# Nine units of experts instead of ten, two of them late, and 415 GB/s in the plan: a hybrid decoder block on one core

## The chip, the cores and the metric

The kernel runs on one core of one Trainium2 chip. The metric is device microseconds of one execution. The kernel before took 536.14 us (median of 3 runs, 535.42 to 536.36); the profiled execution took 535.39 us, and its profile spans 533.4 us from the first to the last instruction, so that 2.0 us lie outside the span.

## What is computed

A decoder block on 256 tokens of width 1024, all float32. A mixer (forgetting attention and gated delta rule, with projections before and behind) comes first. Behind it comes a mixture of 32 experts, of which each token uses two, and behind that a gated embedding and a last norm. The change is all in the part with the experts:

```python
    for e in range(N_EXPERTS):
        hid = jax.nn.silu(t @ w_gate[e]) * (t @ w_up[e])
        out = out + gate[:, e:e + 1] * (hid @ w_down[e])
...
        ple_gate = jax.nn.sigmoid(rmsnorm(x, g_ple[i]) @ w_ple_gate[i])
        x = x + ple_gate * (p[i] @ w_ple_proj[i])
```

`gate` is zero but for two experts a token. Each expert has three weights of 1 MiB (`w_gate`, `w_up`, `w_down`), so that 96 MiB of the weights are the experts'.

## The kernel before, in words

**Places and units.** The kernel does not run every expert on all 256 tokens. It gives an expert a fixed number of places, gathers the tokens routed to it into them by a product with a one-hot matrix `G`, and scatters the result back by a product with the transposed matrix `C`. 128 places make a unit, the 128 columns of one pass through TensorE: two experts of 64 places each, or four of 32. `UNITS` lists them. Before there are ten: (0,1), (2,3), (4,5), (6,7) with 64 places an expert, then (8..11), (12..15) and so on to (28..31) with 32. The first six experts (`NSTAY`) are fixed numbers, since their weights are loaded ahead of the routing; the other numbers are places in an order by load, busiest first, and their weights are fetched by an indirect DMA on GpSimd's queue with the index `idx`. If an expert has more tokens than places, `flag` is set and a loop over all experts (`overflow`, behind a branch that every engine takes) does the rest.

**A unit's work on TensorE.** `group(i)` gathers the features of units 2i and 2i+1 together (`ga<-G,xx`, eight times four products of 128 x 256), and ScalarE copies them to `XT`. `gate_up` multiplies them by the unit's gate tiles (`gate<-`) and up tiles (`up<-`), `hidden` turns the result (`ga<-kp`) and multiplies it by the down tiles in two halves (`dn<-`; for late units the second half is written to `ga`). For an early unit `parts` scatters it into four sums (`sum<-yH,C` and `sum<-yL,C`).

**Late units.** From unit `UE` on a unit is late: units 7, 8, 9 before. Once the early units are summed, the gated embedding's product with `w_ple_gate` starts on those sums alone (`z_early`, `sum<-ra,xx` and the like, 32 products of 128 x 512), while the late units run. What a late unit adds is multiplied by `w_ple_gate` in its 64 places (`z_late`: 16 products `dn<-..,xx` and `gate<-..,xx` of 64 columns, four experts times `FEW` = 16 places), spread back (`z_spread`, `sum<-yH,G`) and added to x by itself (`late_spread`, `ga<-yH,C`). `UL` is the last unit, whose down product comes in three pieces (`last_down`) and whose chain ends the program. `z_early` waits for the gate product of unit `UE` to have been issued, so the first product of the first late unit always stands ahead of it on TensorE.

**Loads.** All weights pass through one ring of tiles of 1 MiB (`Ring`; 20 of them in this part, 17 once three are taken for the embedding), in one order: unit by unit, gate, up, down. A tile is asked for again when the product that read it last has been issued. `w_ple_gate` (four tiles, `wpg0` to `wpg3`) stands in that order right ahead of unit 7 (`WPG`). From unit `UE` - 1 on (`FIRST`) the down tiles come in pieces. SyncE issues the weights loaded ahead, GpSimd the rest, each strictly in order: a transfer whose tile is still in use holds up all behind it. ScalarE and VectorE multiply `w_ple_gate` by `g_ple` when it has come (`scaled`).

**What sets the order.** `Plan` runs the pieces of work as generators and advances the one that can start first by its own account of time, in which every operation has a cost (`Timed.cost`) and a transfer of n bytes takes n / 360e3 us (`Plan.load`). The account sets only the order in which each engine's instructions are written. Nearly all instructions carry line 77, that of the recording helper, so the tiles' names tell them apart.

Of the kernel before, what the change touches and what calls it, by code (L numbers as in the profile page):

```python
# [10 lines left out]
AF = mybir.ActivationFunctionType  # L11
OP = mybir.AluOpType
# [5 lines left out]
D = 1024  # L18
# [2 lines left out]
CAP = 64  # L21


NSTAY, NWIDE = 6, 8
UNITS = [list(range(e, e + 2)) for e in range(0, NWIDE, 2)] + [list(range(e, e + 4)) for e in range(NWIDE, E, 4)]
NU = len(UNITS)

WPG = (7, "g")

UE, UL = NU - 3, NU - 1  # L30

FEW = 16
FIRST = UNITS[UE - 1][0]
# [64 lines left out]
class Plan:  # L98
# [16 lines left out]
        self.end = max(self.end, self.free[key] + self.HOP)  # L115

    def load(self, since, nbytes):
        self.free["D"] = max(self.free["D"], since) + nbytes / 360e3
        return self.free["D"] + 2.0

    def tell(self, name, at=None):
# [2 lines left out]
    def after(self, name, n=1):  # L124
        return lambda: 0.0 if n <= 0 else self.told[name][n - 1] if len(self.told.get(name, ())) >= n else None
# [166 lines left out]
def hybrid_block(tc, x, p_t, w_in, w_o_fox, w_o_delta, w_out, w_gate, w_up, w_down, w_ple_gate,  # L292
# [84 lines left out]
    def K(name):  # L377
        a, b = KEEP[name]
        return kp[:, a:b]
# [849 lines left out]
    def last_tile():  # L1229
        for n in range(2):  # L1230
            yield after("sq1", n + 1)
            turned(1, n)
            yield
        logits(1, 0)
        yield
        yield after("sel")
        rank(0)
        logits(1, 1)
        yield
        yield from ffn_norm(1)  # L1240
        yield
        yield after("parts", 2)

        d = td[:, 0, :].rearrange("p (e s) -> p e s", s=CAP)
        for e in range(4):
            S.activation(d[:, e, :], K("slots"), AF.Square, scale=-1.0, bias=rk[:, 0, e:e + 1])
        S.activation(g0[:, 0].rearrange("p a (e s) -> p (a e) s", s=CAP), d, AF.Relu, scale=-1.0, bias=ones[:, 0:1])
        pr[1] = ps_t("mm")
        P.matmul(pr[1][:, 0:E], ones, sel[:, 0, :], start=True, stop=False)
        busy(6)  # L1250
        for k in range(4):
            gather(0, k)
        yield from route(1)
        rank(1)
        for k in range(4, 8):
            gather(0, k)
        busy(0)
        places(1)
        yield
# [71 lines left out]
    def half(i):  # L1331

        return (i % 2) ^ (i // 2 % 3 == 1)
# [64 lines left out]
    def order_experts():  # L1398
        yield after("sel", 2)
        pt = ps_t("dn")  # L1400
        for t in range(2):
            P.matmul(pt[0:32, 0:32], ones[:, 0:32], sel[:, t], start=t == 0, stop=t == 1)
        for t in range(2):
            P.matmul(pt[0:32, 32:33], sel[:, t], ones[:, 0:1], start=t == 0, stop=t == 1)
        yield
        keys, key, at = so[:, 0:32], so[:, 32:33], so[:, 33:34]
        V.scalar_tensor_tensor(key, pt[0:32, 32:33], 64.0, K("base")[0:32, 32:33], op0=OP.mult, op1=OP.add)
        V.scalar_tensor_tensor(keys, pt[0:32, 0:32], 64.0, K("base")[0:32, 0:32], op0=OP.mult, op1=OP.add)
        V.tensor_scalar(keys, keys, key, None, op0=OP.is_gt)
        V.tensor_reduce(at, keys, axis=AX.X, op=OP.add)  # L1410
        V.tensor_scalar(perm, K("places")[0:32, 0:32], at, None, op0=OP.is_equal)
        yield
        pt = ps_t("dn")
        P.matmul(pt[:, 0:32], K("places")[0:32, 32:33].to_broadcast([32, 128]), perm, start=True, stop=True)
        yield
        V.tensor_scalar(idx, pt[:, 0:32], K("places")[:, 33:34], None, op0=OP.add)
        tell("idx")
        V.tensor_scalar(rowf, pt[:, E - late:E], K("places")[:, 33:34], None, op0=OP.add)
        ring.index, ring.pieces = idx, idp
        ring.pump()  # L1420
        yield
        yield after("gate")
        yield from permute(rk, rkp, K("w_rt")[0:32, 0:256])
        tell("rkp")
        for (a, b), ix in idp.items():
            V.tensor_scalar(ix, rowf, 4.0 / (b - a), float(a // (b - a)), op0=OP.mult, op1=OP.add)
        yield after("weights")
        r = mo.tile([128, 2, 128], F32, name="hidT").rearrange("p k s -> p (k s)")[0:32]
        yield from permute(gr[:, :, :, 1], grp[:, :, :, 1], r)
        V.tensor_copy(grp[:, :, :, 0], gr[:, :, :, 0])  # L1430
        tell("grp")

        V.tensor_scalar(so[:, 34:35], at, NWIDE - 0.5, 32.0, op0=OP.is_lt, op1=OP.mult)
        V.tensor_scalar(so[:, 35:36], at, UNITS[UE][0] - 0.5, float(FEW - 32), op0=OP.is_gt, op1=OP.mult)
        V.tensor_tensor(so[:, 34:35], so[:, 34:35], so[:, 35:36], op=OP.add)
        yield
        pt = ps_t("sum00")
        P.matmul(pt[:, 0:32], so[:, 34:35].to_broadcast([32, 128]), ident[0:32, 0:32], start=True, stop=True)
        yield
        for t in range(2):  # L1440
            V.scalar_tensor_tensor(rko[:, t], rk[:, t], -32.0, pt[:, 0:32], op0=OP.add, op1=OP.subtract)
        V.tensor_reduce(big[:, 0:1], rko.rearrange("p t e -> p (t e)"), axis=AX.X, op=OP.max)
        yield
        pt = ps_t("sum00")
        P.transpose(pt[0:1, 0:128], big[:, 0:1], ident)
        yield
        V.tensor_reduce(big[0:1, 1:2], pt[0:1, 0:128], axis=AX.X, op=OP.max)
        V.tensor_scalar(flag, big[0:1, 1:2], 1.0, None, op0=OP.is_ge)
        tell("flag")
        yield  # L1450
# [16 lines left out]

    def group(i):

        yield after("rows", 2 * i - 2)  # L1470
        yield after("group", i - 1)
        yield after("G", i)
        g = mo.tile([128, 2, 2, 128], F32R, name="G") if i % 2 else g0
        X = XT[:, (slice(0, 2), slice(0, 3, 2), slice(1, 3))[i % 3]]
        wt = mo.tile([128, 2, 2], F32, name="wt", bufs=2)
        QD[i] = (g, wt)
        if i:
            yield after("rkp")
        for t in range(2) if i else (1,):
            yield after("rk", t + 1)  # L1480
            ranks = rkp if i else rk
            if half(2 * i) or 2 * i < UE <= 2 * i + 1:
                for a in range(2):
                    h = half(2 * i + a)
                    one_hot(g[:, t, h:h + 1], ranks[:, t], UNITS[2 * i + a])
            else:
                one_hot(g[:, t], ranks[:, t], UNITS[2 * i] + UNITS[2 * i + 1])
        tell("G")
        yield after("parts", 2)
        yield after("group", i)  # L1490
        yield after("gu", max(0, 2 * i - 1))
        for k in range(8):
            if i:
                yield turn()
                pt = ps_t("ga")[:, 0:256]
                n = 0
                for t in range(2):
                    for part in (xH, xL):
                        P.matmul(pt, part[:, t, k, :], g[:, t].rearrange("p a s -> p (a s)"), start=n == 0, stop=n == 3)
                        n += 1  # L1500
                plan.add(features_of(i, k, X, pt))
            else:
                gather(1, k)
                if k % 2:
                    for kk in (k - 1, k):
                        plan.add(features_of(i, kk, X, xb[kk // 2][:, kk % 2 * 256:kk % 2 * 256 + 256]))
                if k < 7:
                    continue
            yield
        yield after("grp" if i else "weights")  # L1510
        yield turn()

        pt = ps_t("ga")
        for a in range(2):
            u = UNITS[2 * i + half(2 * i + a)]
            m = 128 // len(u)
            for t in range(2):
                for o, e in enumerate(u):
                    P.matmul(pt[o * m:(o + 1) * m, 2 * a:2 * a + 2], g[:, t, a, o * m:(o + 1) * m].bitcast(F32), (grp if i else gr)[:, t, e, :],
                             start=t == 0, stop=t == 1, skip_group_check=True)  # L1520
        yield
        V.tensor_copy(wt.rearrange("p a b -> p (a b)"), pt[:, 0:4])
        tell("wt")
        tell("ga")
        tell("group")
        yield

    def features_of(i, k, X, pt):
        pt = pt.rearrange("p (a s) -> p a s", a=2)
        if True:  # L1530
            S.activation(X[:, :, k], pt, AF.Copy, scale=K("g_ffn")[:, k:k + 1])
        else:
            V.tensor_scalar(X[:, :, k], pt, K("g_ffn")[:, k:k + 1], None, op0=OP.mult)
        tell(f"X{i}")
        if i:
            tell("ga")
        yield
# [598 lines left out]
        nc.sync.dma_start(out[t * 128:(t + 1) * 128, 0:512], th)  # L2136
        yield

    for i in range(NU // 2):
        plan.add(group(i))  # L2140
    plan.add(add_x2())
    plan.add(order_experts())
# [95 lines left out]
```

## Time and profile before

| | |
|---|---|
| median of 3 runs | 536.14 us |
| profiled execution | 535.39 us |
| its span, and its mean granted TensorE clock | 533.4 us, 0.969 |
| TensorE products (PE) busy | 499.9 us, 94% of the span |
| VectorE, ScalarE, GpSimd busy | 229.7, 210.4, 133.9 us |
| moved by DMA | 141.25 MB |

PE is the row of products, PEld that of weight loads beside them. A float32 product shows as two records in the trace, a float32r product as one. Ends of products are modelled, so that a busy PE need not be a PE at its peak. In a table by stretches a row has the length, then for each engine busy us and instructions, and at the end the granted clock, the busy share of the 16 DMA engines and GB/s. In the chain of waits a row has start, length and what ran. In a timeline a row ends with the idle time before the first instruction and what ended it.

### The profile page before, as it was taken

To read this page: it belongs to the slowest core of one execution; us is meant where nothing else is said; L and a number is where in the kernel's file an instruction comes from. 1 tells how busy PE (TensorE), PEld (TensorE's weight loads), DVE (VectorE), ACT (ScalarE), POOL (GpSimd) and SP (SyncE) were. 2 spreads that over 40 slices of the span, in tenths; PEclk is the share of its full clock that TensorE was granted. 3 is DMA by queue.
4 is the path that set the end of the run, shared out by engine and by line. 5 is a ranking of instruction groups with operands and counts; after the bars stand their busy time and mean duration, and the time that the engine had idled before them with its cause. 6 is when DMAs were issued, how large, how long until landed. Compare 5 with 4: busy or idle time off the path is not lost. (4 is left out here: it accounts for less than half of the span.)

```text
span 533.4 us, 10476 instructions
## 1 busy us (share of the span) xinstructions
PE 499.9 (94%) x4375; PEld 351.0 (66%) x4375; DVE 229.7 (43%) x543; ACT 210.4 (39%) x475; POOL 133.9 (25%) x160
## 2 busy tenths in 40 slices
PE   7999999999999999979999999968986999989993
PEld 7999998899999999868555554423543444433441
DVE  3888689764655659584311111100123011012246
ACT  5576845566734545344231221203244011021144
POOL 5000551200000000061233324316444226425000
PEclk9999999999999999998999999979996999998997
DMA  8845533223098569875979999998999996985002
GB/s 343 347 159 167 192 119 115 67 89 131 7 402 303 170 225 423 314 289 188 358 278 384 367 378 340 373 396 308 412 421 416 421 412 227 421 349 201 1 1 79
DMA packets 25605, 141.25 MB, mean 265 GB/s; under 512 B 2625, under 2 KB 2897, under 8 KB 12626
## 3 DMA queue, kind: packets, MB, share of 16 engines
q0 software_dynamic: 14752, 86.01, 41.3%
q1 hardware_dynamic: 10658, 54.01, 27.0%
q8 instruction: 36, 0.59, 0.4%
q10 hardware_dynamic: 144, 0.52, 0.2%
q14 instruction: 15, 0.12, 0.1%
HBM read 139.46 MB, written 1.05 MB: 263 GB/s over the span
## 5 line engine op out<-in xcount | busy, mean ns | idle before, releaser
L77 PE MATMUL mm<-hH,ra 128*128 128x256 f32 x688 | 127.1, 284 | 0.0
L77 PEld LDWEIGHTS mm<-hH,ra 128*128 128x128 f32 x688 | 105.6, 188 | 1.5 <-issue 0.3
L77 PE MATMUL mm<-hL,ra 128*128 128x256 f32 x344 | 83.8, 281 | 0.5 <-DVE hL L77 0.5
L77 PEld LDWEIGHTS mm<-hL,ra 128*128 128x128 f32 x344 | 64.8, 188 | 1.4 <-DVE hL L77 0.7
L77 DVE TENSOR_TENSOR ra<-ra,ra 128x1024 fp32r<-128x1024 f32 x41 | 50.3, 1231 | 18.2 <-ACT ra L77 18.2
L77 ACT CAST ra<-ra 128x1024 fp32r<-128x1024 f32 x41 | 42.9, 1053 | 27.1 <-PE mm L77 23.2
L77 DVE TENSOR_TENSOR yL<-dn,yH 128x512 fp32r<-128x512 f32 x16 | 11.1, 692 | 71.8 <-ACT yH L77 71.8
L77 ACT ACTIVATE XT<-ga,kp 128x256 f32<-128x256 f32 x32 | 15.1, 473 | 55.3 <-PE ga L77 55.3
L77 POOL CAST xx<-xt 128x1024 fp32r<-128x1024 f32 (+1 forms) x2 | 3.3, 1648 | 126.5 <-ACT td L77 123.8
L77 PE MATMUL gate<-ra,XT 128*32 128x256 f32 (+1 forms) x224 | 34.0, 402 | 0.0
L77 PE MATMUL up<-ra,XT 128*32 128x256 f32 (+1 forms) x240 | 33.0, 393 | 0.0
L77 PE MATMUL ga<-G,xx 128*128 128x256 f32 x128 | 23.0, 303 | 7.7 <-PEq L1710 5.1
L77 PE MATMUL gate<-rb,XT 128*32 128x256 f32 (+1 forms) x176 | 30.2, 397 | 0.0
L77 PEld LDWEIGHTS ga<-G,xx 128*128 128x128 f32 x128 | 18.2, 193 | 16.6 <-issue 10.1
L77 DVE SCALAR_TENSOR_TENSOR kp<-th,wt,up 128x256 f32<-128x256 f32 x10 | 4.8, 480 | 52.8 <-PE up L77 52.8
L77 PE MATMUL dn<-ra,hidT 128*32 128x512 f32 (+2 forms) x88 | 23.1, 578 | 0.3 <-DVE rc L77 0.3
L77 PE MATMUL sum<-ra,xx 128*128 128x512 f32 x48 | 22.9, 599 | 0.0
L77 PEld LDWEIGHTS up<-ra,XT 128*32 128x32 f32 (+1 forms) x240 | 14.5, 120 | 11.2 <-issue 5.5
L77 PEld LDWEIGHTS gate<-ra,XT 128*32 128x32 f32 (+1 forms) x224 | 15.0, 124 | 10.2 <-issue 6.1
L77 ACT COPY hidT<-ga 128x256 f32<-128x256 f32 x10 | 3.7, 372 | 40.9 <-PE ga L77 40.9
L77 ACT CAST yH<-dn 128x512 fp32r<-128x512 f32 x16 | 9.3, 583 | 24.1 <-PE dn L77 14.1
L77 PE MATMUL gate<-rc,XT 128*32 128x256 f32 (+1 forms) x64 | 18.0, 416 | 0.0
(477 smaller groups left out, 1097.5 us busy)
## 6 DMA issues: line engine op xcount, KB each, us to landing
ra<-in_w_in SPq DMA_DIRECT2D x19, 1024.0 KB, 5.1
ra<-in_w_gate SPq DMA_DIRECT2D x4, 1024.0 KB, 4.9
ra<-in_w_out SPq DMA_DIRECT2D x3, 1024.0 KB, 4.8
ra<-in_w_up SPq DMA_DIRECT2D x3, 1024.0 KB, 5.0
ra<-in_w_ple_gate POOLq DMA_DIRECT2D x3, 1024.0 KB, 11.1
ra<-in_w_o_fox SPq DMA_DIRECT2D x2, 1024.0 KB, 5.6
rq<-in_w_in SPq DMA_DIRECT2D x2, 1024.0 KB, 10.6
rq<-in_w_down SPq DMA_DIRECT2D x2, 1024.0 KB, 8.1
```

The lines of the kernel that those rows point to most:

```text
L77: return f(*a, **k)
```

## The change

Three things change at once.

- `UNITS` becomes (0,1), (2..5), (6,7), (8..11), ..., (28..31): nine units. Experts 2 to 5 have 32 places instead of 64 and share one unit. With nine units the last group holds one unit, so `group` is written for one too: its gathers are 128 x 128 then.
- `UE` is `NU` - 2 instead of `NU` - 3: units 7 and 8, places 24 to 31, are late. Places 20 to 23 become an early unit. `FIRST` goes from 16 to 20, so that places 16 to 19 get whole down tiles. `w_ple_gate` still stands ahead of unit 7, which now is (24..27): its four tiles are loaded behind the tiles of (20..23) instead of ahead of them.
- `Plan.load` counts 415e3 bytes a us instead of 360e3.

The one-hot matrix of the first group is built by six activations instead of four, and its second half by two operations on VectorE instead of one. `flag` is worked out by four operations more, as the places an expert has are no longer one threshold.

```diff
-NSTAY, NWIDE = 6, 8
-UNITS = [list(range(e, e + 2)) for e in range(0, NWIDE, 2)] + [list(range(e, e + 4)) for e in range(NWIDE, E, 4)]
+NSTAY = 6
+UNITS = [[0, 1], [2, 3, 4, 5], [6, 7]] + [list(range(e, e + 4)) for e in range(8, E, 4)]
...
-UE, UL = NU - 3, NU - 1
+UE, UL = NU - 2, NU - 1
...
-        self.free["D"] = max(self.free["D"], since) + nbytes / 360e3
+        self.free["D"] = max(self.free["D"], since) + nbytes / 415e3
...
-        d = td[:, 0, :].rearrange("p (e s) -> p e s", s=CAP)
-        for e in range(4):
-            S.activation(d[:, e, :], K("slots"), AF.Square, scale=-1.0, bias=rk[:, 0, e:e + 1])
-        S.activation(g0[:, 0].rearrange("p a (e s) -> p (a e) s", s=CAP), d, AF.Relu, scale=-1.0, bias=ones[:, 0:1])
+        d = td[:, 0, :]
+        for i in range(2):
+            m = 128 // len(UNITS[i])
+            for o, e in enumerate(UNITS[i]):
+                S.activation(d[:, 128 * i + o * m:128 * i + (o + 1) * m], K("slots")[:, 0:m], AF.Square, scale=-1.0,
+                             bias=rk[:, 0, e:e + 1])
+        S.activation(g0[:, 0].rearrange("p a s -> p (a s)"), d, AF.Relu, scale=-1.0, bias=ones[:, 0:1])
...
-        V.tensor_scalar(so[:, 34:35], at, NWIDE - 0.5, 32.0, op0=OP.is_lt, op1=OP.mult)
+        x = so[:, 0:1]
+        V.tensor_scalar(x, at, -3.5, None, op0=OP.add)
+        V.tensor_tensor(x, x, x, op=OP.mult)
+        V.tensor_scalar(x, x, 4.0, None, op0=OP.is_gt)
+        V.tensor_scalar(so[:, 34:35], at, 7.5, 32.0, op0=OP.is_lt, op1=OP.mult)
+        V.tensor_tensor(so[:, 34:35], so[:, 34:35], x, op=OP.mult)
...
-                        P.matmul(pt, part[:, t, k, :], g[:, t].rearrange("p a s -> p (a s)"), start=n == 0, stop=n == 3)
+                        P.matmul(pt[:, 0:128 * len(us)], part[:, t, k, :], g[:, t, hs].rearrange("p a s -> p (a s)"),
+                                 start=n == 0, stop=n == 3)
...
-    for i in range(NU // 2):
+    for i in range((NU + 1) // 2):
         plan.add(group(i))
```

Up to the routing no engine's order changes. Behind it three places matter. The first is GpSimd's queue where it starts to fetch the tiles that depend on the routing. In a name such as `rb2_3408` the letters and first digit are the tile of the ring, the rest is a running number. Before:

```order
L209 DMA rb1_3406<-in_w_down,idx_3189 128x2048
L209 DMA rb2_3408<-in_w_gate,idx_3189 128x2048
L209 DMA rq2_3436<-in_w_gate,idx_3189 128x2048
L209 DMA rb0_3438<-in_w_gate,idx_3189 128x2048
L209 DMA rb3_3484<-in_w_gate,idx_3189 128x2048
L209 DMA ra1_3486<-in_w_up,idx_3189 128x2048
```

and after:

```order
L209 DMA rb1_3433<-in_w_down,idx_3191 128x2048
L209 DMA rb2_3435<-in_w_gate,idx_3191 128x2048
L209 DMA rb3_3437<-in_w_gate,idx_3191 128x2048
L209 DMA ra1_3439<-in_w_gate,idx_3191 128x2048
L209 DMA rq2_3471<-in_w_gate,idx_3191 128x2048
L209 DMA rb0_3473<-in_w_up,idx_3191 128x2048
```

The gate product of the second unit gives back `rb1` and `rb2` before, and `rb1`, `rb2`, `rb3` and `ra1` after, so four transfers in a row wait for it instead of two; `rb3` and `ra1` held up tiles of the second unit before and waited for its up product.

The second place is ScalarE ahead of the first late unit, where it scales `w_ple_gate` (the rows of 128x1024) between the copies of the last gathered features (`XT`). Before:

```order
L77 ACTIVATE XT<-ga,kp 128x2x128
L77 ACTIVATE ra_4685<-ra_4685,kp 128x1024
L77 ACTIVATE XT<-ga,kp 128x2x128 x2
L77 CAST C<-ga 128x256
L77 ACTIVATE ra_4687<-ra_4687,kp 128x1024
L77 COPY rb_3800<-sum_3411 128x512
L77 COPY rb_3800<-sum_3412 128x512
L77 CAST G<-ga 128x256
L77 ACTIVATE ra_4689<-ra_4689,kp 128x1024
```

and after:

```order
L77 ACTIVATE XT<-ga,kp 128x128
L77 ACTIVATE ra_4826<-ra_4826,kp 128x1024
L77 ACTIVATE XT<-ga,kp 128x128 x2
L77 ACTIVATE rb_4828<-rb_4828,kp 128x1024
L77 CAST C<-ga 128x256
L77 ACTIVATE rb_4830<-rb_4830,kp 128x1024
L77 COPY rq_3911<-sum_3442 128x512
L77 COPY rq_3911<-sum_3443 128x512
L77 CAST G<-ga 128x256
```

The scalings stand nearly where they stood, the last one three rows further ahead, now among the copies for the one unit of the last group.

The third place is TensorE behind the first late units. Before, between the down product of unit 8 and the gate product of unit 9, the second late unit's turn and spread and a second run of `z_late` (`dn<-..,xx` of 64x512) begin:

```order
L77 MATMUL ga<-kp,G_2747 128x128 x2
L77 MATMUL ga<-kp,rb_3799 128x128 x4
L77 MATMUL ga<-yH,C 128x512
L77 MATMUL ga<-yL,C 128x512
L77 MATMUL dn<-rc_4638,xx_4959 64x512 x2
L77 MATMUL ga<-kp,rb_3799 128x128 x4
L77 MATMUL gate<-rb_5144,XT 32x256
```

After, the one run of `z_late` follows the end of `z_early` and stands ahead of the last unit's down product:

```order
L77 MATMUL sum_5324<-rb_4830,xx_5069 128x512 x2
L77 MATMUL dn<-rc_4790,xx_5069 64x512 x2
L77 MATMUL dn<-ra_4826,xx_5069 64x512 x2
L77 MATMUL dn<-rb_4828,xx_5069 64x512 x2
L77 MATMUL dn<-rb_4830,xx_5069 64x512 x2
L77 MATMUL gate<-rc_4790,xx_5069 64x512 x2
L77 MATMUL gate<-ra_4826,xx_5069 64x512 x2
L77 MATMUL sum_5145<-yH,G 128x512
```

So one gate, up and down product, one spread and one `z_late` are gone between the first late unit and the end; the rows from the last unit's down pieces to the end are the same in number and kind.

More of the change, by code (lines that the diff above doesn't have):

```diff
@@ L1468, in group @@
     def group(i):
+        us = range(2 * i, min(2 * i + 2, NU))
+        hs = slice(half(2 * i), half(2 * i) + 1) if len(us) == 1 else slice(0, 2)
         yield after("rows", 2 * i - 2)
@@ L1481, in group @@
             ranks = rkp if i else rk
[L1482 to L1485, printed above, removed]
-            else:
-                one_hot(g[:, t], ranks[:, t], UNITS[2 * i] + UNITS[2 * i + 1])
+            if i in (1, 3) or half(2 * i) or len(us) == 1:
+                for u in us:
+                    h = half(u)
+                    one_hot(g[:, t, h:h + 1], ranks[:, t], UNITS[u])
+            elif i:
+                one_hot(g[:, t], ranks[:, t], UNITS[2 * i] + UNITS[2 * i + 1])
+            else:
+                for u in us:
+                    one_hot(g[:, t, u:u + 1], ranks[:, t], UNITS[u])
         tell("G")
@@ L1498, in group @@
                     for part in (xH, xL):
-                        P.matmul(pt, part[:, t, k, :], g[:, t].rearrange("p a s -> p (a s)"), start=n == 0, stop=n == 3)
+                        P.matmul(pt[:, 0:128 * len(us)], part[:, t, k, :], g[:, t, hs].rearrange("p a s -> p (a s)"),
+                                 start=n == 0, stop=n == 3)
                         n += 1
-                plan.add(features_of(i, k, X, pt))
+                plan.add(features_of(i, k, X[:, hs], pt[:, 0:128 * len(us)]))
             else:
@@ L1513, in group @@
         pt = ps_t("ga")
-        for a in range(2):
-            u = UNITS[2 * i + half(2 * i + a)]
+        for a in range(2)[hs]:
+            u = UNITS[2 * i + (half(2 * i + a) if len(us) > 1 else 0)]
             m = 128 // len(u)
@@ L1521, in group @@
         yield
-        V.tensor_copy(wt.rearrange("p a b -> p (a b)"), pt[:, 0:4])
+        V.tensor_copy(wt[:, hs].rearrange("p a b -> p (a b)"), pt[:, 2 * hs.start:2 * hs.stop])
         tell("wt")
@@ L1528, in features_of @@
     def features_of(i, k, X, pt):
-        pt = pt.rearrange("p (a s) -> p a s", a=2)
+        pt = pt.rearrange("p (a s) -> p a s", s=128)
         if True:
```

## Prediction

> **What bounds the kernel now.** I read the profile's page first, then the table by stretches from the routing on, then who waited for whom in GpSimd's queue, then the chain of waits.
>
> ```profile
> span 533.4 us, 10476 instructions
> PE 499.9 (94%) x4375; PEld 351.0 (66%) x4375; DVE 229.7 (43%) x543; ACT 210.4 (39%) x475; POOL 133.9 (25%) x160
> ```
>
> PE is busy for 94% of the span, but that is an average over stages. The stretches below are cut at the first unit's gate product (248.8), at the first late unit's (411.4, called G) and at the last unit's last down products (504.6):
>
> ```profile
> core 0: us, PE busy (x) PEld busy (x) DVE busy (x) ACT busy (x) POOL busy (x), PEclk, DMA share, GB/s
> 248.80:350.50 101.70, 101.64 (x811) 52.25 (x810) 19.07 (x65) 25.50 (x60) 33.86 (x36) 1.00 0.89 344
> 269.00:342.40 73.40, 73.40 (x596) 36.74 (x594) 11.10 (x27) 16.47 (x36) 24.48 (x27) 1.00 0.94 363
> 342.40:411.40 69.00, 54.27 (x462) 27.52 (x454) 11.19 (x22) 20.95 (x40) 31.50 (x36) 0.90 0.98 387
> 411.40:440.00 28.60, 28.60 (x195) 12.63 (x198) 2.97 (x5) 2.63 (x5) 9.17 (x10) 0.94 1.01 416
> 411.40:504.60 93.20, 91.26 (x651) 38.25 (x650) 14.66 (x25) 13.10 (x26) 34.10 (x36) 0.96 0.76 299
> 504.60:533.40 28.80, 19.78 (x108) 9.27 (x108) 14.72 (x48) 12.87 (x33) 0.00 (x0) 0.90 0.10 37
> ```
>
> From 411.4 to 504.6 PE has 1.9 us free in 93.2, while DMA moves 299 GB/s of the 416 that it reaches beside it: PE alone bounds this stretch. Before 350.5 PE is full as well, and DMA runs at 344 to 363. So DMA is held back, and GpSimd's queue tells by what:
>
> ```profile
> POOL ra L209 <- PE gate L77: 22.3, 6, 8.1
> POOL ra L209 <- PE up L77: 20.8, 5, 6.8
> POOL rb L209 <- PE gate L77: 12.3, 3, 7.4
> POOL rq L209 <- PEq L1710: 8.6, 1, 8.6
> ```
>
> In each row stand the sum of the waits, their number and the longest. GpSimd waits for PE to hand tiles back, and once, for 8.6 us, at the branch of the overflow (L1710). PE is the bound, and transfers follow it; the tail of 28.8 us is a chain behind the last down pieces.
>
> **The change part by part.** I write the span as G, plus the late stretch (93.2), plus the tail (28.8): 411.4 + 93.2 + 28.8 = 533.4.
>
> *The late stretch loses one unit.* The chain of waits has the three late units' starts and the pieces of one:
>
> ```profile
> 411.49 5.28 PE gate L77 x64
> 447.96 1.00 PE gate L77 x16
> 452.35 7.06 PE sum L77 x16
> 459.41 3.59 PE up L77 x64
> 463.00 1.01 PE dn L77 x4
> 464.45 2.73 PE dn L77 x12
> 467.17 1.72 PE gate L77 x8
> 468.89 1.13 PE sum L77 x4
> 470.01 1.87 PE gate L77 x8
> 471.88 1.85 PE dn L77 x16
> 483.38 1.00 PE gate L77 x16
> 488.28 0.66 PE ga L77 x2
> ```
>
> From the second late unit's gate (447.96) to the third's (483.38) are 35.4 us. The 7.06 of `z_early` in them stay, so a late unit costs at most 28.4. From below: gate and up 2 x 3.59, down 2 x 1.85, `z_late` 1.01 + 2.73 + 1.72 + 1.87 = 7.3, its spread 2 x 1.13, and the spread to x 4 x 0.66, in all 23.1 without the turns between them. I take 27.5, near the upper end, because the stretch itself holds the turns and waits that the sum of pieces lacks. The late stretch becomes 93.2 - 27.5 = 65.7. The tail has the same instructions: 28.8.
>
> *G: PE has the same work, DMA 12 tiles more.* Seven units stand ahead of G before and after: before with 20 experts, after with 24. A unit of two costs PE what a unit of four does:
>
> ```profile
> 248.88 3.67 PE L77 MATMUL gate<-ra,XT 128*64 128x256 f32 x32
> ```
>
> That is 3.67 for 64 places an expert against 3.59 above for 32. So by PE's work G stays at 411.4. But the gate tiles of (24..27) must be there at G now. In the ring's order as much has to come ahead of them as before, `w_ple_gate` included. Before, GpSimd's timeline has two of them asked for here:
>
> ```profile
> 417.04 0.93 POOL L209 DMA_INDIRECT ra<-in_w_gate,idx  x1 [3.60 <-PE gate L77]
> 418.28 0.94 POOL L209 DMA_INDIRECT ra<-in_w_gate,idx  x1 [0.30 <-issue]
> ```
>
> and the table of transfers gives their time to landing:
>
> ```profile
> ra<-in_w_gate,idx POOLq DMA_INDIRECT x2, 9.8
> ```
>
> The first lands at 417.0 + 9.8 = 426.8, the last one tile (1.05 MB at 416 GB/s, 2.5 us) later, at 429.3. From 269.0 until then 73.4 x 0.363 + 69.0 x 0.387 + 17.9 x 0.416 = 60.8 MB moved, at 379 GB/s in the mean. At 416 throughout they take 146.1 us and are there at 415.1. Does DMA reach 416 from 269 on? The gaps come from tiles handed back late:
>
> ```profile
> 268.26 0.94 POOL L209 DMA_INDIRECT rb<-in_w_down,idx  x1 [7.42 <-PE gate L77]
> 269.50 0.94 POOL L209 DMA_INDIRECT rb<-in_w_gate,idx  x1 [0.30 <-issue]
> ...
> 278.57 0.94 POOL L209 DMA_INDIRECT rb<-in_w_gate,idx  x1 [4.75 <-PE up L77]
> ```
>
> Before, the second unit's gate hands back two tiles at 268.3, and the fifth request from there waits for its up product until 278.6. After, that gate hands back four, and the up and down products as well, so each request stands about a unit earlier. Requests 10 us ahead of their landing are what the row with 416 shows (9.8). The branch still blocks GpSimd for its 8.6 us, which requests 10 us ahead cover. I take DMA as full, and G = 416: 415.1, and 0.9 because three paths (tiles, PE at 411.4, `w_ple_gate`) meet within 5 us. The ends for G are 411.4 and 429.3, the pace of now.
>
> The Trainium skill ("DMA: Bandwidth & Descriptors", Specifications) speaks against this: it gives some 358 GB/s as what HBM yields one core. By it the 60.8 MB take 169.8 us, G comes at 438.8, and the change brings nothing; the row with 416 in this trace lies above it.
>
> *`w_ple_gate` loses its cover.* Its three last requests, and the last of ScalarE's four scalings:
>
> ```profile
> L202 POOL DMA_DIRECT2D ra<-in_w_ple_gate x3: 713/713/744, 374.8 to 376.2; - x3
> ...
> DMA to landing us min/median/max: 9.3/10.2/13.0
> ```
>
> ```profile
> 404.60 1.18 ACT L77 ACTIVATE ra<-ra,kp 128x1024 f32<-128x1024 f32 x1
> ```
>
> Its last tile lands at 376.2 + 13.0 = 389.2 and is scaled at 404.6, 6.8 us ahead of G: 15.4 us of cover. After, it lands just ahead of the four gate tiles, at 415.1 - 10.1 = 405.0. Scaling then allows G at 411.8, behind the tiles by 3.3 us: it costs nothing, but ScalarE stands still for it between copies that PE waits for.
>
> *The narrow group.* The last group's 32 products are 128 x 128. No row shows this form. The 64-wide one (from the chain) and the 256-wide one (from the groups by form) bound it:
>
> ```profile
> 505.72 1.01 PE ga L77 x8
> ```
>
> ```profile
> L77 PE MATMUL ga<-G,xx 128*128 128x256 f32 x36 | 6.3, 296 | 0.0
> ```
>
> They are 0.126 and 0.175 us each; if cost grew with width from the first, 0.25. Against 0.175 that is -1.6 to +2.4 us for the 32. I take 0, near the second row.
>
> *The rest at nothing.* The rows of ScalarE and PE around the first one-hot:
>
> ```profile
> 239.95 1.06 ACT L77 ACTIVATE td<-kp,rk 128x64 f32<-128x64 f32 x4 [1.80 <-DVE rs_ffn L77]
> 240.91 2.91 PE L77 MATMUL gate<-ones 128*128 128x128 f32 x12
> 243.47 1.54 PE L77 MATMUL sum<-G,xx 128*128 128x256 f32 x8
> ```
>
> The two activations more are 0.27 each (four take 1.06); twelve filler records on PE up to 243.5 hide them. The operation more for the first one-hot is some 0.1 us on the path. On SyncE the twelve tiles of experts 2 to 5 only change places among themselves, with the same bytes ahead of GpSimd's first fetch. Four more for `flag` run on VectorE, idle there, long before the branch. Four fewer pieces for places 16 to 19 save GpSimd 4 x 1.24 of issuing, which it has to spare.
>
> *The plan's rate* changes nothing up to the routing, and behind it can't be told from the units. It sets products earlier against side work, and PE waits in order if a tile isn't there. I leave PE's idle 14.7 us of 342.4 to 411.4 as they are.
>
> *Sum.* 416 + 65.7 = 481.7; with the tail 510.5; with the 2.0 us outside the span 512.5. All 26.6 + 26.7 + 93.2 x 0.299 = 81.2 MB are there by 269 + 195.2 = 464.2, over 10 us ahead of the last down product. The profiled run (535.39) lies 0.75 under the median (536.14), so I add 0.75: **513 us**.
>
> **The rivals.**
>
> *A: DMA keeps the pace of now.* If something other than tiles held back sets the 379 GB/s, G is 429.3, and the time 429.3 + 65.7 + 28.8 + 2.75 = 526.6. For it: 387 GB/s from 342 to 411, where PE has 14.7 us free. Against: the waits on PE in GpSimd's queue, and 416 as soon as requests run ahead.
>
> *B: slower, the ring starves.* A unit of four holds twelve tiles of the 17 and hands them back in fours, behind which GpSimd's queue stands in order, so requests could come in bursts too late to keep DMA busy. It decides when G passes 536.1 - 2.75 - 28.8 - 65.7 = 438.8, that is under 60.8 / 169.8 = 358 GB/s. At the 344 of the first row G is 445.7 and the time 543. Against: from 342 on the kernel runs units of four alone, at 387 and 416. The Trainium skill's 358 GB/s ("DMA: Bandwidth & Descriptors", Specifications) would put the kernel just at that point.
>
> *C: the change doesn't keep to its places.* If one of experts 2 to 5 had over 32 tokens, the loop of `overflow` would load 32 x 4 times 3 MiB, 384 tiles of 2.5 us, over 900 us. Routing the reference's inputs gives these four 12, 12, 14 and 21 tokens, and the last eight places 11 at most for 16.
>
> **How the numbers follow.** The forecast has 0.78: 506 (G at 411.4, unit 28.4, narrow group -1.6) to 520. A has 0.15, B 0.04, C 0.01, no change 0.02. The forecast alone leaves out 0.22, so the range takes in A: 506 to 527. Faster by over 0.2% (about 1 us, what a measurement can tell): 0.93; same 0.02; slower 0.05.
>
> **What would show it right or wrong.** In the profile after: the gate product with the end of `w_ple_gate` ahead of it near 416, the last down products some 66 us later, and a tail of 28.8. DMA near 416 GB/s from 275 to 415, with few waits on PE in GpSimd's queue there. If G is late and GpSimd waits on PE, A or B holds by the tiles; if GpSimd is ahead and DMA full under 416, DMA itself; if the late stretch is over 68 us, the unit's price was wrong.

## The result, and the profile after

The kernel after takes 514.2 us (median of 4 runs, 512.97 to 515.34) against 536.25 of the kernel before beside it: ratio 0.959, 95% interval 0.956 to 0.962. The forecast was 513, in a range from 506 to 527. The profiled execution took 512.97 us. Two of the ten executions of e1 below lay over 1.5% above its fastest and are left out of its time.

The page of after, its span and the engines' busy time:

```profile
span 510.9 us, 10319 instructions
PE 475.0 (93%) x4313; PEld 339.4 (66%) x4313; DVE 223.8 (44%) x534; ACT 204.0 (40%) x465; POOL 130.3 (26%) x156
```

The span lost 22.5 us, and PE's busy time 24.9: PE stands idle for 35.9 us of the span, before for 33.5. So the gain is work that PE no longer does, and no wait that went.

The table by stretches of after, cut where the prediction cut it (the first two rows are before G, the third is the late stretch, the fourth the tail), and the 8.6 us around G:

```profile
core 0: us, PE busy (x) PEld busy (x) DVE busy (x) ACT busy (x) POOL busy (x), PEclk, DMA share, GB/s
269.00:342.40 73.40, 70.32 (x665) 33.86 (x664) 10.12 (x24) 16.18 (x36) 31.53 (x34) 1.00 0.99 407
342.40:417.90 75.50, 59.89 (x509) 29.19 (x507) 12.67 (x24) 20.84 (x41) 31.15 (x34) 0.89 1.02 416
417.90:482.07 64.17, 63.87 (x429) 27.68 (x428) 7.92 (x13) 7.18 (x14) 24.08 (x26) 0.97 0.77 312
482.07:510.90 28.83, 19.80 (x108) 9.29 (x108) 14.71 (x48) 12.87 (x33) 0.00 (x0) 0.89 0.10 37
411.40:420.00 8.60, 6.36 (x34) 3.53 (x38) 2.58 (x4) 1.17 (x2) 3.35 (x4) 0.50 1.01 421
```

417.9 + 64.2 + 28.8 = 510.9. Ahead of G DMA runs at 407 to 416 GB/s, where before had 363 and 387, and PE now has 3.1 + 15.6 us free there. Until 342.4 the two have changed places as the bound; from there to G PE had 14.7 us free before too, and DMA went from 387 to 416. Behind G PE is full, with 0.3 us free in 64.2.

GpSimd's waits in after, in the prediction's columns:

```profile
POOL rb L209 <- PE gate L77: 11.1, 2, 7.9
POOL ra L209 <- PE up L77: 6.5, 2, 3.3
POOL ra L209 <- PE gate L77: 6.1, 2, 4.5
POOL ra L209 <- DMA rb<-in_w_up,idx: 5.6, 4, 1.5
```

The wait of `ra` for gate products fell from 22.3 to 6.1, that for up products from 20.8 to 6.5; all rows that name a gate, up or down product hold 34.9 us together, before 90.0. New are many rows like the last, short waits put down to a transfer asked for earlier, a sum or a turn (last section). GpSimd's timeline shows the change behind the second unit's gate product, with which the prediction argued:

```profile
268.67 0.94 POOL L209 DMA_INDIRECT rb<-in_w_down,idx  x1 [7.86 <-PE gate L77]
...
273.64 0.94 POOL L209 DMA_INDIRECT rq<-in_w_gate,idx  x1 [0.30 <-PE sum L77]
...
279.08 0.93 POOL L209 DMA_INDIRECT ra<-in_w_up,idx  x1 [3.26 <-PE up L77]
```

The request that waits for the second unit's up product is now the seventh from 268.7 on, at 279.1; before it was the fifth, at 278.6.

The chain of waits of after, at G:

```profile
392.84 15.22 DMA rb<-in_w_ple_gate
408.06 0.78 issue
...
409.89 1.05 ACT rq L77 x2
411.27 1.13 PE ga L77 x4
...
417.97 6.18 PE gate L77 x64
424.16 6.21 PE sum L77 x14
```

The chain goes through the last tile of `w_ple_gate`, its scaling, and the copies that ScalarE has behind that; the first late gate product takes 6.18 us instead of before's 5.28, both at a lowered clock (0.68 from 411.4 to 416.8 us before; 0.50 from 411.4 to 420.0 here, the last row of the table). Whether this chain or the gate tiles set G is tried below.

### The profile page after: what moved, and what is told of

It is laid out like the page before. It is cut to its first block, busy times and chain, and to the rows that moved or that the text cites. A ratio compares the mean times of both kernels' runs of the same rounds, so it can differ in the third digit from the quotient of the medians.

```text
span 510.9 us, 10319 instructions
## 1 busy us (share of the span) xinstructions
PE 475.0 (93%) x4313; PEld 339.4 (66%) x4313; DVE 223.8 (44%) x534; ACT 204.0 (40%) x465; POOL 130.3 (26%) x156
## 3 DMA queue, kind: packets, MB, share of 16 engines
q1 hardware_dynamic: 10658, 54.01, 28.5%
## 4 chain that ended last, share of the span: by engine, by line
PE 76%; DMA 14%; DVE 6%; ACT 2%; issue 1%; POOLq 0%; DVEq 0%; ACTq 0%
PE mm L77 26%; PE sum L77 14%; PE gate L77 8%; PE ga L77 7%; PE dn L77 7%; PE up L77 6%; PE g L77 5%; DMA rb<-in_w_gate,idx 4%; DMA ra<-in_w_up,idx 4%; DMA rb<-in_w_ple_gate 3%; DMA ra<-in_w_down,idp 3%; PE fx L77 2%; DMA xt<-in_x 1%; PE nv L77 1%; ACT td L77 1%
## 5 line engine op out<-in xcount | busy, mean ns | idle before, releaser
L77 PE MATMUL gate<-ra,XT 128*32 128x256 f32 (+1 forms) x224 | 39.0, 420 | 0.0
L77 PE MATMUL up<-ra,XT 128*32 128x256 f32 (+1 forms) x304 | 36.2, 384 | 0.0
L77 ACT ACTIVATE XT<-ga,kp 128x256 f32<-128x256 f32 (+1 forms) x32 | 14.3, 447 | 50.7 <-PE ga L77 50.5
L77 PE MATMUL ga<-G,xx 128*128 128x256 f32 (+1 forms) x128 | 22.8, 301 | 7.7 <-PEq L1724 4.3
L77 PE MATMUL gate<-rq,XT 128*32 128x256 f32 x96 | 26.7, 421 | 0.0
L77 PE MATMUL dn<-ra,hidT 128*32 128x512 f32 (+2 forms) x84 | 25.1, 557 | 1.4 <-DVE yL L77 1.4
L77 PE MATMUL dn<-rq,hidT 128*32 128x512 f32 (+2 forms) x76 | 25.0, 554 | 0.3 <-DVE rb L77 0.3
L77 PE MATMUL dn<-rb,hidT 128*32 128x512 f32 (+1 forms) x68 | 24.9, 600 | 0.0
L77 PEld LDWEIGHTS up<-ra,XT 128*32 128x32 f32 (+1 forms) x304 | 16.3, 115 | 12.2 <-issue 4.9
L77 PE MATMUL sum<-rb,xx 128*128 128x512 f32 x68 | 24.1, 488 | 0.0
L77 PE MATMUL gate<-rb,XT 128*32 128x256 f32 x144 | 21.9, 398 | 0.0
L77 ACT CAST yH<-dn 128x512 fp32r<-128x512 f32 x15 | 8.8, 583 | 31.5 <-PE dn L77 17.7
```

What stands on the lines that cost most here:

```text
L77: return f(*a, **k)
```

## Experiments

Theory: PE's work of one unit went, and the units' tiles now come back in fours, so that DMA runs full and can pay for the twelve tiles more ahead of G. Rivals: the order that the rate of 415 gives, or two late units instead of three. All runs but e9 and e10, which are told below, stand in one table. "PE" is the page's busy time, "idle" the span less that, G the start of the first late gate product in the timeline; the last columns are from the table by stretches: GB/s from 300 to 380 us, and PE's busy us (of 50) and clock from 380 to 430.

| run | time, ratio to before (interval) | span, PE, idle | G | 300-380 | 380-430 |
|---|---|---|---|---|---|
| before | 536.1 to 536.3 | 533.4, 499.9, 33.5 | 411.4 | 361 | 42.5, 0.90 |
| after | 514.2, 0.959 (0.956-0.962) | 510.9, 475.0, 35.9 | 417.9 | 418 | 41.8, 0.86 |
| e1 rate alone | 530.5, 0.989 (0.986-0.992) | 530.3, 501.8, 28.5 | 411.0 | 328 | 45.7, 0.93 |
| e2 rate undone | 513.5, 0.958 (0.956-0.960) | 512.9, 474.8, 38.1 | 420.4 | 419 | 40.7, 0.93 |
| e3 ten units, two late | 528.2, 0.987 (0.983-0.990) | 525.3, 489.0, 36.3 | 426.1 | 346 | 39.4, 0.96 |
| e4 nine units, three late | 533.6, 0.996 (0.994-0.997) | 531.5, 491.6, 39.9 | 388.0 | 416 | 36.7, 0.83 |
| e5 `w_ple_gate` earlier | 514.0, 0.960 (0.957-0.963) | 510.8, 476.1, 34.7 | 418.5 | 417 | 41.0, 0.97 |
| e6 one late unit | 517.8, 0.965 (0.963-0.967) | 516.3, 475.1, 41.2 | 441.0 | 418 | 42.0, 0.88 |
| e7 `w_ple_gate` 4 tiles later | 509.0, 0.949 (0.946-0.952) | 504.8, 473.3, 31.5 | 412.2 | 418 | 45.3, 0.96 |
| e8 8 tiles later | 509.7, 0.950 (0.947-0.953) | 505.7, 471.8, 33.9 | 409.9 | 418 | 43.6, 1.00 |
| e11 e7's edit on before | 538.4, 1.004 (1.002-1.006) | 536.8, 499.9, 36.9 | 406.8 | 358 | 45.4, 0.97 |
| e12 e4, `w_ple_gate` 12 later | 527.3, 0.984 (0.980-0.988) | 523.2, 487.7, 35.5 | 384.8 | 418 | 42.0, 0.86 |

**e1, the rate alone**, on the kernel before:

```diff
-        self.free["D"] = max(self.free["D"], since) + nbytes / 360e3
+        self.free["D"] = max(self.free["D"], since) + nbytes / 415e3
```

> The kernel before with 415 GB/s in the plan instead of 360 and nothing else (ten units, three late ones). Theory (the unit that is gone brings the gain, the rate next to nothing): 534 to 538 us, G (start of the first late unit's gate products) within 2 us of the 411.4 of before. Rival (the order that the rate gives brings it): 514 to 524 us, with G or the late stretch shorter by over 10 us.

530.5 us: neither. The order alone is worth 5.6 us with ten units, and the theory had put it at nothing. PE's work is the same, 1.9 us longer even; its idle time fell by 5.0 us in the profiled execution:

```profile
380.00:430.00 50.00, 45.67 (x443) 21.99 (x436) 10.62 (x22) 15.60 (x30) 25.55 (x28) 0.93 1.02 415
```

Before has 42.50 busy in this stretch, so PE waits 3.2 us less around G, although DMA was slower ahead of it (328 against 361 GB/s). Which moved product does it was not isolated.

**e2, the rate undone**: the same line the other way, on the kernel after.

> The kernel after with 360 GB/s in the plan: nine units and two late ones as in after, the old rate. Theory (the unit that is gone brings the gain): 512 to 517 us, G within 2 us of 417.9. Rival (the rate brings it): 526 to 536 us.

513.5 us, as the theory had it; G was 0.5 us outside its bounds. With nine units the rate is worth nothing that can be measured, so taking it away from after loses none of the 22 us, though it is worth 5.6 with ten units.

**e3, two late units and all ten units**, on e1's kernel (`C2`, the storage for the late one-hot, moves to a matrix that is free by then):

```diff
-WPG = (7, "g")
+WPG = (8, "g")
-UE, UL = NU - 3, NU - 1
+UE, UL = NU - 2, NU - 1
```

> Two late units, but all ten units kept (experts 2 to 5 in two units of two as before), 415 GB/s in the plan. Theory (the gain is one unit's products less, wherever they stand): the late stretch falls to 64 to 66 us, but the eighth unit stands ahead of G, where TensorE or the transfers pay for it: G 426 to 432, time 520 to 528 us. Rival (a late unit is dear, an early one cheap, so that two late units bring the gain by themselves): G 411 to 420, time 507 to 516 us.

528.2 us with G at 426.1: the theory's side, not the rival's, if 0.2 us past the theory's upper bound. PE does 10.9 us less than before and 12.8 less than e1, which has the same rate, so a unit costs it that much less early than late. But the late stretch is 70.4 us (the last down products start at 496.5), not 64 to 66. The timeline at G has most of the difference:

```profile
426.07 0.97 PE L77 MATMUL gate<-ra,XT 128*32 128x256 f32 x2 [1.20 <-DMA ra<-in_w_gate,idx]
428.56 1.06 PE L77 MATMUL gate<-rb,XT 128*32 128x256 f32 x2 [1.52 <-DMA rb<-in_w_gate,idx]
431.05 1.06 PE L77 MATMUL gate<-ra,XT 128*32 128x256 f32 x2 [1.42 <-DMA ra<-in_w_gate,idx]
433.54 0.64 PE L77 MATMUL gate<-ra,XT 128*32 128x256 f32 x2 [1.43 <-DMA ra<-in_w_gate,idx]
```

Four waits of 5.6 us together, each for one gate tile: with ten units DMA brought 346 GB/s, and the twelve tiles more ahead of G are late.

**e4, nine units and three late ones**, on the kernel after:

```diff
-WPG = (7, "g")
+WPG = (6, "g")
-UE, UL = NU - 2, NU - 1
+UE, UL = NU - 3, NU - 1
...
-        yield after("rows", i + 1)
+        yield after("rows", max(i + 1, 8))
...
+        for t in range(2):
+            yield after(f"a{t}", n + 1)
```

(The last two edits hold back work that would otherwise meet storage still in use.)

> Nine units as in after, but three late ones as in before (experts 20 to 23 late too, with 16 places; w_ple_gate one unit earlier), 415 GB/s in the plan. Theory (the merge alone brings the gain; ahead of G the transfers set the pace, 12 tiles of 1 MiB at 2.5 us or 30 us a unit, behind it TensorE, 29 us a unit, so that the border can be moved at no cost): G 386 to 391, late stretch 92 to 95, time 511 to 518 us. Rival (two late units bring the gain): 528 to 538 us.

533.6 us: the theory failed, and the rival's number holds here. G came at 388.0 as the theory had it, 30 us sooner, but the last down products only at 502.7, so the late stretch is 114.7 us and not 93. Two things were wrong. G is a place in the order and not a sum of work done: what PE still owed to the early units now stood behind it. And PE waits there for transfers:

```profile
393.43 0.62 PE L77 MATMUL up<-rb,XT 128*32 128x256 f32 x2 [1.33 <-DMA rb<-in_w_up,idx]
396.01 0.62 PE L77 MATMUL up<-rc,XT 128*32 128x256 f32 x2 [1.96 <-DMA rc<-in_w_up,idx]
398.50 0.63 PE L77 MATMUL up<-ra,XT 128*32 128x256 f32 x1 [1.87 <-DMA ra<-in_w_up,idx]
```

The stretch from 380 to 430 shows the effect, 13.3 us free and the clock at 0.83:

```profile
380.00:430.00 50.00, 36.66 (x304) 18.08 (x304) 9.17 (x18) 11.89 (x24) 22.66 (x25) 0.83 1.02 417
```

**e10 and e12** ask how much of that the waits are: e4 with `WPG = (7, "g")`, so that the first late unit's twelve tiles come 10 us sooner.

> Nine units with three late ones (533.6 us when w_ple_gate stood ahead of the first late unit's gate tiles), w_ple_gate now 12 tiles later, behind the first late unit's twelve. Theory (a late unit is 12 us dearer on TensorE than an early one, and the run with three late ones paid some 10 us more for waits on transfers ahead of and behind G and for products at a lowered clock after them; these waits now go): 522 to 529 us. Rival (the dearer late unit alone accounts for it): 531 to 535 us.

e10 took 555.8 us, and the kernel before beside it 556.7, both slower than they were elsewhere, by 28 and 20 us, for a reason that isn't known (last section), and the ratio of 1.002 (0.996 to 1.008) settles nothing. Once more:

> Nine units, three late ones, w_ple_gate behind the first late unit's twelve tiles, once more (the first time the transfers were disturbed, as for the kernel before beside it). Theory (the waits for transfers of the run with three late units go): 522 to 529 us, ratio 0.974 to 0.987. Rival (the dearer late unit alone accounts for its 533.6 us): 531 to 535 us.

527.3 us, as the theory had it, 6.2 under e4. PE's busy time and the stretch of e12:

```profile
PE 487.7 (93%) x4363; PEld 343.8 (66%) x4363; DVE 227.7 (44%) x542; ACT 207.5 (40%) x472; POOL 133.6 (26%) x160
```

```profile
380.00:430.00 50.00, 42.02 (x318) 21.14 (x322) 12.04 (x23) 13.82 (x26) 22.00 (x24) 0.86 1.02 414
```

PE is busy 5.4 us more in that stretch than in e4. With the same idle time as after (35.5 and 35.9), e12 has 12.7 us more of PE's work and a span 12.3 us longer: that is the price of a unit being late instead of early.

**e5, `w_ple_gate` earlier**: `WPG = (6, "g")` on the kernel after, so that its scaling is long done at G.

> The kernel after with the four tiles of w_ple_gate one unit earlier in the order of transfers, ahead of experts 20 to 23 (their scaling then lies well ahead of G). The same bytes stand ahead of the first late unit's gate tiles. Theory (the bytes set G: those tiles land at 411 to 419 us as now): G 416 to 418, time 512 to 514.5 us. Rival (the landing of w_ple_gate and its scaling, last in the chain of waits of the run after, set G): G 408 to 411, time 505 to 508 us.

514.0 us, G at 418.5, 0.5 above the theory's bounds. So `w_ple_gate` and its scaling, though last in the chain of after, did not set G by themselves: with them out of the way the same bytes bring G as late. The four gate tiles end there: the first was asked for at 400.3 and landed 10.7 us later, at 411.0, and three more at 2.5 us each make 418.5, which is G. In after the same sum is 395.4 + 15.8 + 7.5 = 418.7, within 0.8 of its G.

**e6, one late unit**, on the kernel after (with the same kind of edit to `C2`, and one more, by which the turns of the last unit's pieces wait until `z_early` is issued far enough):

```diff
-WPG = (7, "g")
+WPG = (8, "g")
-UE, UL = NU - 2, NU - 1
+UE, UL = NU - 1, NU - 1
```

> The kernel after with one late unit instead of two (experts 24 to 27 in the early manner, with 32 places; w_ple_gate ahead of the gate tiles of 28 to 31). Two late units instead of three took 10.9 us from TensorE's busy time with ten units, 16.6 us with nine. Theory (what is left is set by the transfers, which bring 12 tiles more ahead of G at 2.5 us each): G 446 to 450, time 511 to 519 us, no better than after. Rival (TensorE's work sets the time all along): 498 to 505 us.

517.8 us, in the theory's range, but its G, the first gate product, came at 441.0 and not at 446 to 450. The timeline:

```profile
441.00 1.06 PE L77 MATMUL gate<-ra,XT 128*32 128x256 f32 x2 [2.19 <-DMA ra<-in_w_gate,idx]
443.49 1.06 PE L77 MATMUL gate<-xx,XT 128*32 128x256 f32 x2 [1.43 <-DMA xx<-in_w_gate,idx]
445.97 1.06 PE L77 MATMUL gate<-rc,XT 128*32 128x256 f32 x2 [1.42 <-DMA rc<-in_w_gate,idx]
448.47 0.64 PE L77 MATMUL gate<-ra,XT 128*32 128x256 f32 x2 [1.44 <-DMA ra<-in_w_gate,idx]
```

The four gate tiles come 2.5 us apart, with DMA full; PE waits for each, and the last comes at 448.5, where the theory had put G. PE's busy time didn't fall (475.1): its records are 50 fewer, but the mean granted clock of the span is 0.949 and not 0.967, and the gate products from 441.0 to 454.4 keep PE busy for 9.1 us at 0.52. Its idle time rose by 5.3 us. As built here, two late units is the better place for the border; how much of the loss the added wait makes was not tried.

**e7 and e8, `w_ple_gate` later**: `WPG = (7, "u")` (behind the four late gate tiles) and `WPG = (7, "d")` (behind the up tiles too), on the kernel after.

> The kernel after with the four tiles of w_ple_gate moved four tiles later, behind the first late unit's gate tiles and ahead of its up tiles. Theory (G waits for bytes; TensorE idles some 7 us between 404 and 418 us in the run after): those gate tiles land 10 us earlier, at 401 to 409 us, the gate products (6.3 us at a lowered clock in the run after) move into that idle time, and z_early's products, which need w_ple_gate (now in at 419 us, scaled by 422), start at about 422 to 424 as now: time 508 to 512.5 us. Rival (w_ple_gate is what the rest waits for, so later is worse): 516 to 521 us.

509.0 us, as the theory had it, and the fastest of all: ratio 0.949 against after's 0.959, with intervals apart. The stretch around G and that from 480 us on, and G itself in the timeline:

```profile
380.00:430.00 50.00, 45.34 (x360) 21.97 (x361) 10.16 (x20) 13.49 (x26) 21.73 (x24) 0.96 1.02 415
...
480.00:540.00 60.00, 15.83 (x66) 6.99 (x62) 14.11 (x47) 11.76 (x30) 0.00 (x0) 0.94 0.05 17
```

```profile
411.65 0.66 PE L77 MATMUL ga<-kp,rq 128*128 128x128 f32 x4 [0.79 <-DVE xx L77]
412.23 0.40 PE L77 MATMUL gate<-rc,XT 128*32 128x256 f32 x1
```

The gate products now fill gaps between the turned features (`ga<-kp,rq`), 5.7 us sooner. PE is busy 3.6 us more in this stretch than in after, its idle time falls by 4.4 us over the span, its work by 1.7. (The profiled execution of e7 lies 2.4 us under its median, that of after 1.2, so some of this is the choice of execution.) `z_early` starts at 417.5, sooner than the theory's 422 to 424, and G at 412.2 is near the 411.4 at which the prediction put PE's own work.

> The kernel after with w_ple_gate eight tiles later, behind the first late unit's up tiles. Theory: gate and up products come 10 us earlier, but w_ple_gate lands at about 429 us and z_early's 27 us of products start at about 432 instead of 424, with 6 us of gate and up products moved ahead of them: 512 to 519 us. Rival (TensorE has enough other work until then): 506 to 511 us.

509.7 us: the rival. The timeline has the first product of `z_early` right behind the up products:

```profile
421.03 0.59 PE L77 MATMUL up<-rb,XT 128*32 128x256 f32 x2
421.73 1.13 PE L77 MATMUL sum<-rb,xx 128*128 128x512 f32 x2
```

It did not start at 432 but at 421.7, since it takes `w_ple_gate` tile by tile as it comes, and the theory had let it wait for the last one. Between e7 and e8 there is no difference to be measured.

**e9 and e11**: e7's edit on the kernel before.

> The kernel before (ten units, 360 GB/s in the plan) with the one edit of the faster run of the kernel after: w_ple_gate behind the first late unit's gate tiles. Theory (the move pays only where the transfers are what G waits for; ahead of G in the run before TensorE has work and the transfers run at 363 to 387 GB/s): 534 to 537.5 us, as before. Rival (the move is worth 5 us wherever it is made): 529 to 532 us.

e9 was slow like e10, 553.4 us against 556.7 (ratio 0.997, 0.993 to 1.001). Once more:

> The kernel before with w_ple_gate behind the first late unit's gate tiles, once more (the first time the transfers of this kernel and of the kernel before fell to 230 GB/s in some slices, and both took 553 to 557 us; ratio 0.997, between 0.993 and 1.001). Theory (the move pays only where G waits for transfers): ratio 0.997 to 1.001. Rival (worth 5 us wherever it is made): ratio 0.988 to 0.993.

538.4 us, ratio 1.004 (1.002 to 1.006): nothing gained, a little lost, so the rival falls, and the theory's 0.997 to 1.001 is missed by a little. Its reason is wrong too. Two stretches of e11:

```profile
380.00:430.00 50.00, 45.38 (x368) 23.50 (x368) 9.06 (x19) 15.05 (x27) 20.62 (x23) 0.97 1.02 417
...
480.00:540.00 60.00, 41.82 (x312) 18.15 (x311) 20.37 (x57) 17.06 (x41) 9.93 (x10) 0.92 0.28 102
```

and of before:

```profile
380.00:430.00 50.00, 42.50 (x400) 22.87 (x399) 9.53 (x20) 14.59 (x27) 20.96 (x23) 0.90 1.02 418
...
480.00:540.00 60.00, 44.12 (x308) 18.86 (x306) 20.95 (x58) 16.84 (x41) 7.03 (x8) 0.91 0.18 63
```

Around G the move pays here as well: PE is busy 2.9 us more, and G is 4.6 us sooner. It is given back from 480 us on, where PE is free for 56.8 - 41.8 = 15.0 us of what is left of the span, against 53.4 - 44.1 = 9.3. e7, with two late units, had no such loss (24.8 - 15.8 = 9.0 free there). The traces show where: `z_early` ends at 451.7 in e11 and at 459.4 in before. From there until the last down products (508.0 and 504.6) PE is free for 8.4 us in e11 and for 2.0 in before. So the later units' turns have no products of `z_early` left to stand beside them. That this costs the time was not tried by itself.

## Why the prediction was right, point by point

**The sum.** G 416, measured 417.9; late stretch 65.7, measured 64.2; tail 28.8, measured 28.8; 2.0 outside the span, measured 2.1. That the span of 510.5 came out at 510.9 is in part luck: G was put 1.9 us too early and the late stretch 1.5 too long. The median lay 1.2 us above the profiled run, where 0.75 was added.

**The late stretch.** The unit's price, 27.5 between 23.1 and 28.4, came out at 93.2 - 64.2 = 29.0, above its upper end, which was called the most that it can be, by 0.6. It is right only as a difference between two kernels with the same work ahead of their markers, seven units each. It is not what one late unit costs: e4 and e12 show that G moves by 30 to 33 us when a unit crosses it while the span changes by 12 to 21. Told by PE's work, the 24.9 us are one unit that is gone (e12, 12.2 under before) and one that is early instead of late (after, 12.7 under e12).

**G, and rival A.** "I take DMA as full" held: 407 and 416 GB/s from 269 us on, where before had 363 and 387. Every run of the table with nine units has 416 to 419 from 300 to 380 us, every one with ten 328 to 361, whatever the rate and the number of late units. Tiles that came back late had held DMA back, as GpSimd's waits said. The tiles still came later than the 415.1 of the prediction, the last at 418.7: until 342.4 DMA was at 407 and not 416 (1.6 us), and from 269 on it moved 73.4 x 0.407 + 75.5 x 0.416 + 0.8 x 0.421 = 61.6 MB and not 60.8 (1.9 us). The Trainium skill's 358 GB/s for HBM and one core ("DMA: Bandwidth & Descriptors", Specifications) would have put the kernel at no gain. The 407 and 416 of this one core lie above it, and the measurement decides.

**The two halves.** At the same rate of 415 four runs differ by one half each: e1 (ten units, three late), e3 (ten, two late), e12 (nine, three late; `w_ple_gate` at the same place among the transfers as in after) and after (nine, two late). PE's work adds up: a unit early instead of late takes off 12.8 us with ten units and 12.7 with nine, the merge 14.1 with three late units and 14.0 with two. The time doesn't add up (times are medians, idle times are of one execution each). Against e1 the border alone brings 2.3 us (e3) and the merge alone 3.2 (e12; against before 8 and 9, the rate included), as PE's idle time grows by 7.8 and 7.0; the other half then brings 14.0 or 13.1 with the idle time as it was. So neither half does much alone. In e3 5.6 us of the idle time are the waits for gate tiles; that these would make up the difference is an account and was not tried, and for e12 the cause is open.

**`w_ple_gate`.** Forecast to land at 405.0 and to cost nothing, its last tile landed at 408.8 (asked for at 392.8 and 15.9 us to landing), late like the gate tiles behind it. e5 agrees that its scaling costs nothing. What the prediction did not look at is where it stands in the transfers: its 10 us ahead of the gate tiles cost 5 us (e7).

**The narrow group.** Put at 0 between -1.6 and +2.4. The groups by form of after:

```profile
L77 PE MATMUL ga<-G,xx 128*128 128x256 f32 x96 | 17.6, 306 | 6.3 <-PEq L1724 4.3 <-ACT XT L77 1.1 <-ACT C L77 0.5
L77 PE MATMUL ga<-G,xx 128*128 128x128 f32 x32 | 5.2, 284 | 1.4 <-ACT XT L77 0.9 <-ACT hidT L77 0.5
```

17.6 / 96 = 0.18 us for a wide product and 5.2 / 32 = 0.16 for one of half the width, so that it saves 0.7 us: near nothing.

**The branch.** "Requests 10 us ahead cover" its 8.6 us: DMA did not stop there (418 GB/s from 340 to 380 us, with PE held up until 351.7), and GpSimd's waits of after have no row for it. PE lost 4.3 us at it (L1724 in the row above).

**The plan's rate.** "Changes nothing up to the routing, and behind it can't be told from the units": e2 has it at nothing with nine units, e1 at 5.6 us with ten. Reading it as nothing was right for this kernel and no rule.

**Rivals B and C** did not come: from 269 us to G no row of the table is under 407 GB/s, and a span of 510.9 us has no room for the loop of the overflow.

## What to carry to other kernels

When a change turns a stage from bound by an engine to bound by transfers, look again at the order of the transfers in that stage: here a move of four tiles was worth 5 us after the change, while the same move in the kernel before was given back later. A border such as G between two stages is a place in the instructions; price a move across it by each engine's whole busy and idle time, not by the distance between markers. And two halves of a change can each be worth little by themselves: here the work that one took off PE turned into idle time, until the other was there.

## What the runs showed of the hardware that was not expected

GpSimd got no more than some eight transfers ahead. The table of transfers of after from 310 to 352 us (the number asked for and the median time to landing), and GpSimd's timeline there:

```profile
rb<-in_w_down,idx POOLq DMA_INDIRECT x4, 19.5
ra<-in_w_down,idx POOLq DMA_INDIRECT x3, 19.6
```

```profile
322.20 0.94 POOL L209 DMA_INDIRECT rq<-in_w_gate,idx  x1 [1.56 <-DMA rb<-in_w_up,idx]
324.70 0.94 POOL L209 DMA_INDIRECT ra<-in_w_gate,idx  x1 [1.56 <-PE sum L77]
327.19 0.94 POOL L209 DMA_INDIRECT ra<-in_w_gate,idx  x1 [1.55 <-DMA ra<-in_w_up,idx]
```

It asks for a tile every 2.5 us, the pace at which they land, and each lands 19.5 us later: 19.5 / 2.5 = 7.8 are under way. The releasers named change from row to row, and neither a transfer that lands nor a sum gives back a tile of the ring, so a limit on what may be outstanding fits better than any of them; it was not tried by itself.

The granted clock was 0.50 from 411.4 to 420.0 us in after, and the gate products at G took 6.18 us. In e5 it was 1.00 from 408 to 418 and still so over the gate products. From 380 to 430 PE is busy for about as long in both (41.8 and 41.0 us), but just ahead of G, from 408 to 418, for 5.5 us in after and 8.0 in e5. The lower clock goes with the longer idle time right before it; whether that lowers it was not tried.

In one batch of runs, made on chip 13 where the other experiments ran on three others, every kernel was slow: the kernel before took 556.7 us, e9 553.4 and e10 555.8. The expectations of e11 and e12 put this down to transfers, since e9 has slices at 230 GB/s. Its trace doesn't bear that out. GpSimd stands still for an up product there, and does so in e11 nearly as long (e9 above, e11 below):

```profile
441.04 0.94 POOL L209 DMA_INDIRECT ra<-in_w_up,idx  x1 [17.86 <-PE up L77]
436.17 0.94 POOL L209 DMA_INDIRECT ra<-in_w_up,idx  x1 [15.12 <-PE up L77]
```

From 440 to 460 us e9 has 212 GB/s and e11 245, and both come to over 410 where requests run ahead. What e9 has and e11 has not is idle time of PE that ends with nothing that the profile shows, 8.5 us in these rows against 0.7:

```profile
PE ga L77 <- issue: 2.6, 4, 1.2
PE gate L77 <- issue: 2.5, 5, 0.8
PE dn L77 <- issue: 2.5, 1, 2.5
PE g L77 <- issue: 0.9, 1, 0.9
```

PE's busy time is 9.2 us longer too, for the same 4375 records. Whether it was the chip or the moment, and what held PE up, is open; the kernel before has no trace from there. A ratio to a kernel that ran beside it is of use in such a case, a time is not.
